# Loading the first tile of a mean-subtract-square kernel in eight pieces, on every eighth partition

## The chip, the core and the metric

The kernel runs on one NeuronCore of a Trainium2 chip. The metric is the device time of one execution in microseconds (us), taken as the median of several runs. One execution is also recorded by the hardware profiler; its record, the trace, is what the pages and tables below are read from. The core's on-chip memory, SBUF, has 128 partitions. Data comes from HBM and goes back to it by DMA, on 16 DMA engines that all DMAs of the core share.

## The reference

For each of the 1024 rows of a 1024 x 4096 float32 matrix, the mean of the row is subtracted from every element and the difference is squared:

```python
def reference(x, axis):                 # x: (1024, 4096) float32, axis = -1
    mean = np.mean(x, axis=axis, keepdims=True)
    return ((x - mean) ** 2).astype(np.float32)
```

Input and output are 16 MiB each (16.78 MB in the units of the profile).

## The kernel before

The matrix is cut into two tiles of 512 rows. In a tile each partition holds four consecutive rows of x, that is 64 KiB in one piece: partition p of tile 0 holds rows 4p to 4p+3. Both tiles are loaded at the start, each by one DMA over all 128 partitions, issued from SyncE (SP). Then, one row per partition at a time, VectorE (DVE) sums the row with negated sign, divides by 4096, and ScalarE (ACT) computes the square of x plus that bias, in place. After each second row the finished half of the tile (128 partitions x 32 KiB, 4 MiB) is stored by one DMA. Both tiles have their own buffer, so nothing waits for a buffer to come free.

```python
    Q = 4                                # rows per partition in a tile
    H = 2                                # rows per store
    ntiles = B // (P * Q)                # 1024 / 512 = 2

    x_t = x.rearrange("(n p q) d -> n p (q d)", p=P, q=Q)
    out_t = out.rearrange("(n p q) d -> n p (q d)", p=P, q=Q)
    # ... pools: one buffer per tile ...

    for i in range(ntiles):
        x_tile = io.tile([P, Q * D], F32)
        nc.sync.dma_start(out=x_tile, in_=x_t[i])          # L43
        tiles.append(x_tile)

    for i in range(ntiles):
        for q in range(Q):
            row = tiles[i][:, q * D:(q + 1) * D]
            # ... neg_sum, neg_mean: [P, 1] each ...
            nc.vector.reduce_sum(out=neg_sum, in_=row,     # L51
                                 axis=mybir.AxisListType.X, negate=True)
            nc.vector.tensor_scalar_mul(out=neg_mean, in0=neg_sum, scalar1=inv_d)   # L54
            nc.scalar.activation(out=row, in_=row,         # L55
                                 func=mybir.ActivationFunctionType.Square,
                                 bias=neg_mean, scale=1.0)
            if q % H == H - 1:
                part = slice((q + 1 - H) * D, (q + 1) * D)
                nc.sync.dma_start(out=out_t[i][:, part], in_=tiles[i][:, part])     # L64
```

Of the kernel before, what the change touches and what calls it, by code (L numbers as in the profile page):

```python
# [2 lines left out]

os.environ.setdefault("NEURON_RT_ULTRASERVER_MODE", "4")

# [4 lines left out]

F32 = mybir.dt.float32


@with_exitstack
def kernel(
    ctx: ExitStack,
    tc: tile.TileContext,
    x: bass.AP,
    axis: bass.AP,
    out: bass.AP,  # L20
):


    nc = tc.nc

    B, D = x.shape
    P = nc.NUM_PARTITIONS
    Q = 4
    H = 2
    assert B % (P * Q) == 0  # L30
    ntiles = B // (P * Q)
    inv_d = 1.0 / float(D)

    x_t = x.rearrange("(n p q) d -> n p (q d)", p=P, q=Q)
    out_t = out.rearrange("(n p q) d -> n p (q d)", p=P, q=Q)

    io = ctx.enter_context(tc.tile_pool(name="io", bufs=ntiles))
    stats = ctx.enter_context(tc.tile_pool(name="stats", bufs=2 * ntiles * Q))

    tiles = []  # L40
    for i in range(ntiles):
        x_tile = io.tile([P, Q * D], F32)
        nc.sync.dma_start(out=x_tile, in_=x_t[i])  # L43
        tiles.append(x_tile)

    for i in range(ntiles):
        for q in range(Q):
            row = tiles[i][:, q * D:(q + 1) * D]
            neg_sum = stats.tile([P, 1], F32)
            neg_mean = stats.tile([P, 1], F32)  # L50
            nc.vector.reduce_sum(  # L51
                out=neg_sum, in_=row, axis=mybir.AxisListType.X, negate=True
            )
            nc.vector.tensor_scalar_mul(out=neg_mean, in0=neg_sum, scalar1=inv_d)  # L54
            nc.scalar.activation(  # L55
                out=row,
                in_=row,
                func=mybir.ActivationFunctionType.Square,
                bias=neg_mean,
                scale=1.0,  # L60
            )
            if q % H == H - 1:
                part = slice((q + 1 - H) * D, (q + 1) * D)
                nc.sync.dma_start(out=out_t[i][:, part], in_=tiles[i][:, part])  # L64


# [1 line left out]
_INS = ['x', 'axis']  # L68
_OUTS = [((1024, 4096), 'float32')]

_NUMBERS = {'axis': -1}


# [26 lines left out]
```

## Time and profile before

| | before |
|---|---|
| time, median of 3 runs (lowest, highest) | 83.3 us (83.25, 83.38) |
| span of the profiled execution | 81.3 us |
| moved by DMA | 16.78 MB read, 16.78 MB written |
| loads | 2 DMAs of 8 MiB |
| stores | 4 DMAs of 4 MiB |
| DVE busy | 35.4 us (44%) |
| ACT busy | 30.7 us (38%) |

The span is the recorded stretch from the first to the last instruction; the measured time is 2.0 us longer. The profile has a line of DMA activity in 40 slices: one digit per slice for the share of time in which the 16 DMA engines had a packet in work, and a line with what they moved, in GB/s. A packet is counted where it ends, so the single GB/s values jump; a table of longer stretches gives the rate more smoothly. In that table each line is a stretch of time with the busy time of the compute engines in it, the DMA share (1.00 is all 16 engines busy all the time) and the rate. "SPq" is the queue of SyncE, from which the DMAs are issued. The chain of waits follows the work that ended last back to the start.

### The profile page before, as it was taken

How to read it: one execution, taken by the hardware profiler on the slowest of the kernel's cores; microseconds unless marked ns; L12 is line 12 of the kernel's file. 1: busy time of each engine (PE TensorE's matmuls, PEld its weight loads, DVE VectorE, ACT ScalarE, POOL GpSimd, SP SyncE). 2: the span in 40 equal slices, each digit the busy share in tenths (PEclk: the TensorE clock that was granted, in tenths of full speed). 3: DMA queues.
4: the chain of work that ended last, by engine and by line, in shares of the span. 5: the costliest groups of instructions: out<-in, count | busy, mean ns of one | idle time of the engine just before them, and what ended most of it. 6: DMA issues, size and time to landing. Idle time of an engine off the chain costs nothing.

```text
span 81.3 us, 79 instructions
## 1 busy us (share of the span) xinstructions
DVE 35.4 (44%) x16; ACT 30.7 (38%) x9; POOL 0.2 (0%) x4
## 2 busy tenths in 40 slices
DVE  0000000000099999999749999999920000000000
ACT  0000000000060005969699930979879980000000
POOL 0000000000000000000000000000000000000000
DMA  9399947999965999992997997997998998898990
GB/s 387 129 516 516 516 193 322 516 516 516 516 290 226 516 516 516 516 483 129 419 516 306 467 516 322 451 516 338 435 516 354 419 516 387 387 516 387 403 500 0
DMA packets 864, 33.55 MB, mean 413 GB/s; under 512 B 96, under 2 KB 96, under 8 KB 96
## 3 DMA queue, kind: packets, MB, share of 16 engines
q1 hardware_dynamic: 864, 33.55, 96.2%
HBM read 16.78 MB, written 16.78 MB: 412 GB/s over the span
## 4 chain that ended last, share of the span: by engine, by line
DMA 50%; DVE 22%; ACT 5%; ACTq 4%; SPq 0%; issue 0%
DMA x_tile<-in_x_dram 50%; DVE neg_sum L51 21%; ACT x_tile L55 5%; ACTq L95 4%; SPq L43 0%; DVE neg_mean L54 0%
## 5 line engine op out<-in xcount | busy, mean ns | idle before, releaser
L51 DVE TENSOR_REDUCE neg_sum<-x_tile 128x1 f32<-128x4096 f32 x8 | 35.0, 4413 | 24.1 <-DMA x_tile<-in_x_dram 24.1
L55 ACT ACTIVATE x_tile<-x_tile,neg_mean 128x4096 f32<-128x4096 f32 x8 | 29.4, 3704 | 13.5 <-DVE neg_mean L54 13.5
L55 ACT ACT_TABLE_LOAD x1 | 1.3, 1283 | 22.5 <-DMA x_tile<-in_x_dram 22.5
L54 DVE TENSOR_SCALAR neg_mean<-neg_sum 128x1 f32<-128x1 f32 x8 | 1.1, 148 | 0.0
L81 POOL MEMSET const-bfloat16-1.0<- 128x1 bf16 x1 | 0.1, 101 | 0.0
L81 POOL MEMSET const-uint8-127<- 128x1 uint8 x1 | 0.1, 101 | 0.0
L81 POOL MEMSET const-float32-0.0<- 128x1 f32 x1 | 0.1, 98 | 0.2 <-issue 0.2
L81 POOL MEMSET const-float32-1.0<- 128x1 f32 x1 | 0.1, 98 | 0.0
## 6 DMA issues: line engine op xcount, KB each, us to landing
out_dram<-x_tile SPq DMA_DIRECT2D x4, 4096.0 KB, 12.9
x_tile<-in_x_dram SPq DMA_DIRECT2D x2, 31.2
```

Source lines behind the costliest of these rows:

```text
L51: nc.vector.reduce_sum(out=neg_sum, in_=row, axis=mybir.AxisListType.X, negate=True)
L54: nc.vector.tensor_scalar_mul(out=neg_mean, in0=neg_sum, scalar1=inv_d)
L55: nc.scalar.activation(out=row, in_=row, func=mybir.ActivationFunctionType.Square, bias=neg_mean, scale=1.0,)
L81: nc = _bacc.Bacc("TRN2", target_bir_lowering=False, num_devices=1)
L95: with _tile.TileContext(nc) as tc:
```

## The change

Tile 0 is now loaded by eight DMAs instead of one. DMA g (g = 0 to 7) reads one contiguous MiB of x, rows 64g to 64g+63, as 16 pieces of 64 KiB, and lays them on the 16 partitions g, g+8, g+16, ..., g+120. So partition 8e+g of tile 0 now holds rows 4(16g+e) to 4(16g+e)+3. The stores of tile 0 follow the same map on the side of HBM, with an access pattern of 16 x 8 x 8192 elements. Tile 1, its load and its stores are as before, and so is all arithmetic. The change is for the HBM side of the load: each DMA reads one unbroken MiB, and its pieces are spread over the whole height of SBUF.

```diff
+    G = 8
+    E = P // G
...
+    x_g = x[:P * Q, :].rearrange("(g e q) d -> g e (q d)", g=G, e=E, q=Q)
+    out_g = out[:P * Q, :].rearrange("(g e q) d -> e g (q d)", g=G, e=E, q=Q)
...
-        nc.sync.dma_start(out=x_tile, in_=x_t[i])
+        if i == 0:
+            for g in range(G):
+                nc.sync.dma_start(out=x_tile[g::G, :], in_=x_g[g])
+        else:
+            nc.sync.dma_start(out=x_tile, in_=x_t[i])
...
-                nc.sync.dma_start(out=out_t[i][:, part], in_=tiles[i][:, part])
+                dst = out_g[:, :, part] if i == 0 else out_t[i][:, part]
+                nc.sync.dma_start(out=dst, in_=tiles[i][:, part])
```

## The prediction, made before the changed kernel ran

> **What bounds the kernel now.** I read the head of the page first: spans, busy shares, and the DMA line in 40 slices.
>
> ```profile
> span 81.3 us, 79 instructions
> DVE 35.4 (44%) x16; ACT 30.7 (38%) x9; POOL 0.2 (0%) x4
> DMA  9399947999965999992997997997998998898990
> q1 hardware_dynamic: 864, 33.55, 96.2%
> HBM read 16.78 MB, written 16.78 MB: 412 GB/s over the span
> ```
>
> No compute engine is busy for half of the span; the DMA engines are busy for 96.2% of it. That alone doesn't say that they set the end, so next I cut the span where loads and stores change over and asked for the table of stretches (columns: stretch, length, busy time of DVE, ACT and POOL, clock, DMA share, GB/s):
>
> ```profile
> 2.20:5.70 3.50, 0.00 (x0) 0.00 (x0) 0.00 (x0) 1.00 0.79 337
> 5.70:22.60 16.90, 0.10 (x1) 0.05 (x1) 0.00 (x0) 1.00 1.00 434
> 22.60:41.90 19.30, 17.68 (x9) 10.43 (x4) 0.00 (x0) 1.00 0.94 407
> 41.90:61.30 19.40, 17.64 (x8) 14.79 (x5) 0.00 (x0) 1.00 1.00 432
> 61.30:80.70 19.40, 0.00 (x0) 5.45 (x2) 0.00 (x0) 1.00 0.94 405
> ```
>
> The load of tile 0 runs at 434 GB/s with share 1.00 once it has started, the stores of tile 0 (41.9 to 61.3) at 432 GB/s, also with share 1.00. (The 407 and 405 come from where packets are counted: each of these stretches also moves 8 MiB in 19.3 or 19.4 us.) So four blocks of 8 MiB follow each other at one rate: 8.389 MB / 434 GB/s = 19.3 us each, 4 x 19.3 = 77.3 us. What is left of 81.3 is about 2.2 us ahead of the first packet, 0.6 us of a slow first round (the stretch to 5.7 us) and about 0.7 us at the end.
>
> The chain of waits and the queue's own waits say whether compute ever delays a store:
>
> ```profile
> 0.73 0.38 SPq L43
> 1.16 40.64 DMA x_tile<-in_x_dram
> 41.83 8.75 DVE neg_sum L51 x2
> ```
> ```profile
> 39.46 27.65 SPq L64 DMA_DIRECT2D out_dram<-x_tile  x4
> ```
>
> The first store is issued at 39.46 us, before the second load has landed (41.8 us), and the last at 66.8 us, while the stores ahead of it still move. The queue never runs dry. The end is set by bytes over rate, not by the DVE and ACT steps that the chain names between 41.8 and 63 us.
>
> [...]
>
> [...]
>
> [...]
>
> [...]
>
> **The change, part by part.**
>
> *Load of tile 0.* Sixteen rows to 16 engines: all engines work, one 64 KiB piece each per DMA. But the partitions are p = 8e + g. [...]Estimate: half of 434, that is 217 GB/s; 8.389 MB / 217 = 38.7 us in place of 19.3: **+19.3 us**, all on the path, as the DMA engines set the end.
>
> *Stores of tile 0.* The HBM side is now 16 x 8 x 8192 elements, the SBUF side 128 x 8192. [...]Two stores, 8.389 MB, at 216 instead of 432 GB/s: **+19.4 us**. This step rests on my reading of how such a pattern is dealt out, so it is less sure than the first.
>
> *More DMAs.* Seven more issues of about 0.4 us (0.38 us above) are done by 0.73 + 8 x 0.4 = 4 us, beside transfers that last to 40 us: 0 on the path. The built program has eight completion semaphores for its DMAs, so the load of tile 1, the ninth DMA, waits until the first MiB has landed, at 6 to 8 us; by then seven more MiB are in the queue, at least 17 us of work. 0 on the path. DVE's first reduction waits for eight semaphores in place of one, also beside the load of tile 1.
>
> *Packets.* Load pieces stay at 64 KiB and store pieces at 32 KiB, so their number stays 256 + 512; there are 7 x 16 = 112 more completion packets. In the page all packets together, completions too, fill 96.2%, and no gap shows where two DMAs meet; I count 0.1 us.
>
> *Does a late load starve the stores?* Tile 0 lands at 22.5 + 19.3 = 41.8 us, tile 1 at 61.1. The first store would be issued at 39.5 + 19.3 = 58.8, still ahead of 61.1. Tile 1's last store is issued near 66.8 + 19.4 = 86.2, while the stores of tile 0 move until 61.1 + 38.8 = 99.9. No new gap. Sum: 81.3 + 19.3 + 19.4 + 0.1 = 120.1 us of span, 122.1 us of time.
>
> **The rivals.**
>
> *Only the loads slow down.* [...]the time is 83.3 + 19.4 = 102.7 us. For it: the SBUF side of the store is still 128 partitions. Against: the HBM side no longer is.
>
> *Engines drift apart.* [...]Then the load costs 10 to 15 us more and the stores as well: 103 to 113 us. Against: equal pieces and a start within half a microsecond make them march together.
>
> [...]nothing changes but the issue: 83.3 us, or 82.7 if contiguous reads also remove the slow first round (0.6 us). [...]A gain over 2% (1.7 us) would need more than the whole of that slow round[...].
>
> **Range and chances.** I give both conflicts 0.6 (116 to 124 us), one alone or drift 0.25 (98 to 113), no conflict 0.13, faster 0.02. [...]I say 121 us. The range, 100 to 124.5, takes in the loads-only case. Faster 0.02, same 0.13, slower 0.85.
>
> **What would show it.** Right: from about 6 to 41 us the DMA share stays at 1.00 while the rate is near 217 GB/s, and DVE starts near 42 instead of 22.5 us; from 42 to 61 the load of tile 1 is back at 434; from 61 to 100 the stores of tile 0 show 216; from 100 on 432 again. DVE and ACT durations (4413 and 3704 ns) don't change. Wrong: 434 GB/s from 6 us on[...]; 432 from 61 us on[...]; a rate between that rises towards the end of the first load (drift); a low DMA share, which would mean waiting for issue or semaphores instead of slow packets.

## The result: half as long again

The changed kernel takes 124.84 us (median of 6 runs, 123.86 to 125.06), the kernel before 83.32 us (6 runs, 83.25 to 83.4). The ratio is 1.4966, with a 95% interval of 1.4918 to 1.5013: 41.5 us more.

First the head of its page, to be held against the head shown in the prediction:

```profile
span 123.3 us, 97 instructions
DVE 35.4 (29%) x16; ACT 30.7 (25%) x9; POOL 0.2 (0%) x4
q1 hardware_dynamic: 976, 33.56, 95.1%
HBM read 16.78 MB, written 16.78 MB: 272 GB/s over the span
```

DVE and ACT did the same work in the same time. The same bytes went through 16 DMA engines that were as busy as before (95.1%, before 96.2%), but the rate fell from 412 to 272 GB/s. This is the line to remember: an engine that is held up counts as busy. Each packet just takes longer: in the records of single packets a 64 KiB piece of tile 0 takes 5.11 us, before 2.42. The extra 112 packets are the completions of seven more DMAs, 7 x 16.

The timeline of the changed kernel (columns: start, length, then what) says when the tiles arrived:

```profile
0.73 5.08 SPq L51 DMA_DIRECT2D x_tile<-in_x_dram  x8
8.85 0.35 SPq L53 DMA_DIRECT2D x_tile<-in_x_dram  x1
44.42 8.75 DVE L61 TENSOR_REDUCE neg_sum<-x_tile 128x1 f32<-128x4096 f32 x2 [44.42 <-DMA x_tile<-in_x_dram]
61.38 27.35 SPq L75 DMA_DIRECT2D out_dram<-x_tile  x4
63.45 8.74 DVE L61 TENSOR_REDUCE neg_sum<-x_tile 128x1 f32<-128x4096 f32 x2 [1.32 <-DMA x_tile<-in_x_dram]
```

DVE gets tile 0 at 44.42 us instead of 22.50, tile 1 at 63.45 instead of 41.83. Tile 0 comes 21.9 us late, and tile 1 as good as keeps that delay (21.6 us): between the two lie 19.0 us, before 19.3. The load of tile 1 is issued late, at 8.85 us, because it waits for the first MiB (3.0 us in the queue's own waits), but with seven MiB still queued that costs nothing. The first store is issued at 61.38 us, ahead of the last load again.

The table of stretches of the changed kernel, cut at those points, shows the rates (last column GB/s, before it the DMA share). A packet counts in the stretch in which it starts, not, as said above, in which it ends:

```profile
6.80:42.50 35.70, 0.00 (x0) 0.00 (x0) 0.00 (x0) 1.00 1.00 206
42.50:62.70 20.20, 17.71 (x8) 9.36 (x4) 0.00 (x0) 1.00 0.99 415
62.90:82.00 19.10, 17.71 (x8) 14.79 (x5) 0.00 (x0) 1.00 0.93 206
82.00:102.40 20.40, 0.00 (x0) 6.37 (x2) 0.00 (x0) 1.00 1.00 259
102.40:122.30 19.90, 0.00 (x0) 0.00 (x0) 0.00 (x0) 1.00 0.83 357
120.10:123.30 3.20, 0.00 (x0) 0.00 (x0) 0.00 (x0) 1.00 0.02 10
```

The last stretch of the same length in the kernel before:

```profile
78.10:81.30 3.20, 0.00 (x0) 0.00 (x0) 0.00 (x0) 1.00 0.38 164
```

Tile 0 is loaded at 206 GB/s with share 1.00. Tile 1 loads at 415. The stores of tile 0 begin at 206 and come to 259 in their second half (which holds some of tile 1's stores). In the last line is something new: in the last three microseconds only a few engines still start a packet.

### The profile page after: what moved, and what is told of

Its sections match the earlier page's. It is cut to its first block, busy times and chain, and to the rows that moved or that the text cites. A ratio compares the mean times of both kernels' runs of the same rounds, so it can differ in the third digit from the quotient of the medians.

```text
span 123.3 us, 97 instructions
## 1 busy us (share of the span) xinstructions
DVE 35.4 (29%) x16; ACT 30.7 (25%) x9; POOL 0.2 (0%) x4
## 3 DMA queue, kind: packets, MB, share of 16 engines
q1 hardware_dynamic: 976, 33.56, 95.1%
## 4 chain that ended last, share of the span: by engine, by line
DMA 32%; DVE 29%; SPq 3%; ACT 3%; ACTq 3%; another core or an unknown queue 1%; issue 0%; DVEq 0%
DMA x_tile<-in_x_dram 32%; DVE neg_sum L61 28%; SPq L51 3%; ACT x_tile L65 3%; ACTq L106 3%; DVE neg_mean L64 0%; DVEq L61 0%
```

## The experiments

The theory: the partitions that the 16 engines work on at one moment set the rate. Sixteen with a step of 8, as in the load, get half of the 434 GB/s; the stores get as little because, by my estimate, their pattern leads the engines to such partitions as well. The recorded texts call that a conflict. Why such partitions should be slow no trace shows. The rivals: the HBM side (all engines inside one MiB), the number of DMAs, and, for the stores, engines brought out of step by the load. In all of them only tile 0's transfers are edited, starting from the kernel before; times stand beside runs of the kernel before on the same chip (83.23 to 83.29 us). The ratios leave out single executions more than 1.5% above the fastest of their kernel, so they can differ a little from the quotient of two medians.

### The loads alone, with the old rows

```diff
-        nc.sync.dma_start(out=x_tile, in_=x_t[i])
+        if i == 0:
+            for g in range(8):
+                nc.sync.dma_start(out=x_tile[g::8, :], in_=x_t[0][g::8, :])
```

> The load of tile 0 is eight DMAs onto partitions g, g+8, ..., as in the changed kernel, but each partition keeps the rows it had before, so a DMA reads 16 pieces of 64 KiB that lie 512 KiB apart in HBM in place of one unbroken MiB; the stores are those of the kernel before. [...]the reads don't matter, the partitions do. DVE starts near 44.4 us as in the changed kernel, the stores run at 432 GB/s, the time is 83.3 + 21.9 = 105.2 us. Rival, HBM locality (16 engines reading inside one MiB slow each other down): DVE starts near 22.5 us and the time is near 83.5 us. Rival, number of DMAs: [...]the runs on 128 partitions and on 16 partitions in a row tell it apart.

Measured: 104.77 us, 1.258 times the kernel before (1.255 to 1.260), 21.5 us more. From its timeline and its table of stretches:

```profile
44.41 8.74 DVE L55 TENSOR_REDUCE neg_sum<-x_tile 128x1 f32<-128x4096 f32 x2 [44.41 <-DMA x_tile<-in_x_dram]
```
```profile
6.80:42.50 35.70, 0.00 (x0) 0.00 (x0) 0.00 (x0) 1.00 1.00 207
62.70:82.00 19.30, 17.71 (x8) 15.00 (x5) 0.00 (x0) 1.00 1.00 433
```

Reads 512 KiB apart or in one unbroken MiB: DVE starts at 44.41 or 44.42 us. So the order of reads in HBM has no part in the loss. The stores here are at 433 GB/s, so what slowed them in the changed kernel is not the load before them.

### The same MiBs on 16 partitions in a row

```diff
+                nc.sync.dma_start(out=x_tile[16 * g:16 * g + 16, :],
+                                  in_=x_t[0][16 * g:16 * g + 16, :])
```

> The load of tile 0 is eight DMAs of one contiguous MiB each, onto 16 partitions in a row (16g to 16g+15), rows and stores as before. [...]tile 0 lands near 80 us, the time is 141 to 147 us. Rivals, HBM locality or number of DMAs: the reads and the count are those of the changed kernel, so DVE starts at 44.4 us and the time is near 105 us.

Measured: 139.07 us, 1.670 times (1.666 to 1.674). The stretch that lies inside the load of tile 0:

```profile
10.00:75.00 65.00, 0.00 (x0) 0.00 (x0) 0.00 (x0) 1.00 0.98 111
```

Same count of DMAs, same size, each reading one unbroken MiB as in the changed kernel, and the rate about halves again. It is a little better than the 141 to 147 us that I expected: 111 GB/s is 0.54 of the changed kernel's 206, where 206 is 0.47 of 434.

### Eight DMAs over all 128 partitions

```diff
+            for g in range(8):
+                c = slice(2048 * g, 2048 * g + 2048)
+                nc.sync.dma_start(out=x_tile[:, c], in_=x_t[0][:, c])
```

> The load of tile 0 is eight DMAs of one MiB each, all over 128 partitions with 8 KiB a partition, rows and stores as before. [...]434 GB/s, DVE starts near 22.6 us, the time is 83.2 to 84 us. Rival, number of DMAs (issue, completion, the wait of the ninth for the first): the time rises by a good part of the 21.9 us by which tile 0 came late in the changed kernel, to 95 us or more.

Measured: 84.75 us, 1.018 times (1.016 to 1.020). The number of DMAs is not the cause. The 1.5 us are more than I had allowed; its timeline says where they are lost:

```profile
22.80 4.42 DVE L56 TENSOR_REDUCE neg_sum<-x_tile 128x1 f32<-128x4096 f32 x1 [0.36 <-DMA x_tile<-in_x_dram]
43.19 8.74 DVE L56 TENSOR_REDUCE neg_sum<-x_tile 128x1 f32<-128x4096 f32 x2 [15.78 <-DMA x_tile<-in_x_dram]
```

The last piece of tile 0 comes only 0.3 us late, tile 1 then 1.4 us late. So the loss falls into the load of tile 1, which is unchanged, but here the first store is issued at 21.23 us and waits behind it. In the records of single packets the last 16 pieces of that load take 3.35 to 3.77 us each instead of 2.42. That the waiting stores slow them is a guess, not shown.

### The stores alone

```diff
+                    dst = out[:P * Q, :].rearrange("(g e q) d -> e g (q d)",
+                                                   g=8, e=16, q=Q)[:, :, part]
```

> Loads as in the kernel before, stores of tile 0 with the 16 x 8 x 8192 pattern of the changed kernel, so the rows of tile 0 come out in another order. Theory: [...]near 216 GB/s instead of 432, and they alone cost 18.5 to 20.5 us, with the ends of the 16 engines spread by 2 to 3 us: 102 to 104 us. If the extra of this run and that of the loads alone add up to the 41.5 us of the changed kernel, the two are separate. Rival: the stores of the changed kernel were slow because the conflict of the load had brought the engines out of step; then this run is near 83.5 us.

Measured: 103.26 us, 1.236 times (1.229 to 1.244), 20.0 us more. 21.5 + 20.0 = 41.5: the two parts add up to the whole of the changed kernel. Its table of stretches, first the load, then the stores of tile 0, then the end:

```profile
5.70:22.60 16.90, 0.00 (x0) 0.00 (x0) 0.00 (x0) 1.00 1.00 434
42.50:80.00 37.50, 17.34 (x8) 19.96 (x6) 0.00 (x0) 1.00 0.98 247
97.00:101.10 4.10, 0.00 (x0) 0.00 (x0) 0.00 (x0) 1.00 0.06 24
```

The stores are slow behind a load at full rate, but at 247 GB/s, not 216 (the stretch holds some of tile 1's stores too). And the end is ragged: share 0.06 over the last 4.1 us. The engines drift apart in these stores: until 67 us their 32 KiB packets take anything from 1.2 to 2.8 us, before 1.21. The packets fill 93.4% of the span of 101.1 us, 94.4 us of each engine; before they filled 78.2 of 81.3. So the packets cost 16.2 us more, not 19.4. But 6.7 us are idle instead of 3.1, and these 3.6 us lie at the end, where the engines that are done don't take over what is left to the others.

### Loads on two kinds of partition sets in one kernel

```diff
+            spans = [slice(32 + j, 96, 4) for j in range(4)]
+            spans += [slice(j, 32, 2) for j in range(2)]
+            spans += [slice(96 + j, 128, 2) for j in range(2)]
+            for g in range(8):
+                nc.sync.dma_start(out=x_tile[spans[g], :], in_=x_g[g])
```

> The load of tile 0 is eight DMAs of one contiguous MiB on 16 partitions each, as in the changed kernel; the first four go to partitions 32+j, 36+j, ..., 92+j (j = 0 to 3)[...], the last four to every second partition of 0 to 31 and of 96 to 127[...]. Stores of the kernel before, so the rows of tile 0 come out in another order. [...]the first 4 MiB at 434 GB/s (until about 12.5 us), the next 4 MiB at 205 GB/s (20.5 us more), DVE starts near 33.3 us, the time is 83.3 + 10.8 = 94.1 us. Rivals, HBM locality or DMAs of 16 partitions as such: no difference between the halves, DVE starts near 44.4 us, the time is near 105 us.

Measured: 94.41 us, 1.133 times (1.131 to 1.136). Timeline, then the stretches of the first four and the last four DMAs:

```profile
33.84 8.74 DVE L59 TENSOR_REDUCE neg_sum<-x_tile 128x1 f32<-128x4096 f32 x2 [33.84 <-DMA x_tile<-in_x_dram]
```
```profile
5.70:12.60 6.90, 0.00 (x0) 0.00 (x0) 0.00 (x0) 1.00 1.25 427
12.60:33.30 20.70, 0.00 (x0) 0.00 (x0) 0.00 (x0) 1.00 0.92 212
```

This is the clearest of the runs. Eight DMAs of one kind, 16 partitions and one unbroken MiB each; four run at 427 GB/s and four at 212, and only the choice of partitions sets them apart. (The first share is over 1 because whole packets are counted where they start.) In the records of single packets the first set takes 2.42 us for 64 KiB once started, the second mostly 5.11, the same as in the changed kernel.

### Stores on the same two kinds of sets

```diff
+                    for g in range(8):          # the same spans
+                        nc.sync.dma_start(out=out_g[g][:, part],
+                                          in_=tiles[i][spans[g], part])
```

> Loads of the kernel before; each of the two stores of tile 0 is cut into eight DMAs of 16 partitions, [...]each writes 16 pieces of 32 KiB inside one MiB of HBM (64 KiB apart), as in the changed kernel, so the rows of tile 0 come out in another order. [...]in each half store 2 MiB at 432 GB/s (4.9 us) and 2 MiB at about 207 GB/s (10.1 us), so 5.3 us more for each, the time is near 93.5 to 95 us. Rival, HBM writes inside one MiB are slow: no difference between the DMAs, near 103 us. Rival, small DMAs wait for issue: the DMA share falls below 1.

Measured: 95.15 us, 1.140 times (1.132 to 1.147), just over what I expected. The two halves of the first store, then of the second:

```profile
41.90:46.60 4.70, 4.64 (x2) 4.70 (x2) 0.00 (x0) 1.00 1.10 397
46.60:57.00 10.40, 10.40 (x5) 6.50 (x3) 0.00 (x0) 1.00 0.91 233
57.00:61.00 4.00, 2.67 (x3) 3.32 (x2) 0.00 (x0) 1.00 1.09 418
61.00:71.00 10.00, 0.00 (x0) 5.88 (x2) 0.00 (x0) 1.00 0.96 239
```

Fast, slow, fast, slow, with the same kind of HBM writes throughout. The partitions matter for reading SBUF (397 and 418 GB/s against 233 and 239) as they do for writing it (427 against 212), and 16 engines writing inside one MiB of HBM are not slow.

### Contiguous reads without the conflict

```diff
+            x_q = x[:P * Q, :].rearrange("(q p) d -> q p d", p=P, q=Q)
+            for q in range(Q):
+                nc.sync.dma_start(out=x_tile[:, q * D:(q + 1) * D], in_=x_q[q])
...
+                    out_q = out[:P * Q, :].rearrange("(q p) d -> p q d", p=P, q=Q)
+                    # store out_q[:, q + 1 - H:q + 1, :]
```

> What the change was for, without the conflict: the load of tile 0 is four DMAs of two contiguous MiB each, over all 128 partitions, one row of 16 KiB per partition; the stores of tile 0 follow that map. [...]contiguous reads bring nothing, [...]and all stays at the rate of before: 83.0 to 84.5 us, though DVE starts near 8 us because its first reduction needs only the first DMA. Rival, contiguous reads are worth something: below 82 us.

Measured: 84.54 us, 1.016 times (1.013 to 1.018). What the change was for brings nothing even without its price. Nor does compute that starts at 8.33 us: the queue of bytes is as long as before. The 1.3 us lost look like those of the run with eight DMAs over 128 partitions: here too stores wait early, and the last 16 pieces of tile 1's load take 2.70 to 3.63 us.

### A store pattern of 8 x 16

```diff
+                    dst = out[:P * Q, :].rearrange("(g e q) d -> e g (q d)",
+                                                   g=16, e=8, q=Q)[:, :, part]
```

> As the run of the stores alone, but the HBM side of the stores of tile 0 is 8 x 16 x 8192 elements: partition 16e+g holds rows of block (g, e), e = 0 to 7, g = 0 to 15 (rows of tile 0 come out in another order). [...]only 8 engines work, [...]the 8.39 MB take 81 us in place of 19.4, time near 145 us. If they drift apart as in the run with 16 x 8, up to a third less: not under 120 us. Rival, the scattered HBM writes are what costs: as with 16 x 8, near 103 us. Rival, 8 engines with no conflict[...] (217 GB/s): also 103 us, but with half of the packets missing from the second eight engines, so the DMA share would be 0.5; the rate per busy engine tells it.

Measured: 144.89 us, 1.734 times (1.723 to 1.746). From its page, and a stretch early in tile 0's stores:

```profile
DMA packets 848, 33.55 MB, mean 233 GB/s; under 512 B 80, under 2 KB 80, under 8 KB 80
```
```profile
44.00:58.00 14.00, 14.00 (x6) 10.07 (x3) 0.00 (x0) 1.00 0.49 108
```

80 completion packets where the kernel before has 96, 16 for each DMA: that fits two DMAs with 8 completions each, on 8 engines only. Share 0.49 is half of the engines, and at 108 GB/s each of the eight gets 13.5, half of the 27.1 of an engine before. So these eight are slow themselves; at the rate of before they would reach 8 x 27.1 = 217 GB/s, by estimate. The time fits too (145 was expected). Over 43 to 119 us the share is 0.65 and the rate 179 GB/s: by my reading the other eight engines have gone on to tile 1's stores, and the rates mix.

### The load in two queues

```diff
+                issuer = nc.sync if g < 4 else nc.scalar
+                issuer.dma_start(out=x_tile[g::8, :], in_=x_t[0][g::8, :])
```

> The loads of the run with partitions 8e+g and old rows, but g = 0 to 3 are issued from SyncE and g = 4 to 7 from ScalarE[...]. If [...]half of the engines start with the one and half with the other, the conflict goes: tile 0 lands near 23 us, time 83.5 to 86 us. If all engines alternate in step, both sets still take turns: 104 to 105.5 us as with one queue. In between if they drift.

Measured: 103.86 us, 1.249 times (1.246 to 1.252). The engines stay in step: in the records of single packets all 16 take a piece of the one queue, then all 16 a piece of the other. So they alternate between the partitions of g = 0 to 3 and those of g = 4 to 7, and the conflict stays: DVE starts at 43.39 us. The 0.9 us saved on the 104.77 of one queue are in the packets, which take 4.93 us in place of 5.11.

### One load DMA with the pattern of the stores

```diff
+            x_e = x[:P * Q, :].rearrange("(g e q) d -> e g (q d)", g=8, e=16, q=Q)
+            nc.sync.dma_start(out=x_tile, in_=x_e)
```

> The load of tile 0 is one DMA over 128 partitions whose HBM side is 16 x 8 x 16384 elements, the pattern of the changed kernel's stores; stores of the kernel before, so the rows of tile 0 come out in another order. Theory[...]: the load is slow with one DMA too, DVE starts near 44 us and the time is near 105 us, or some us less if the engines drift apart as they do in the stores. Rival ([...]the slow stores have another cause): DVE starts near 22.5 us, time near 83.4 us.

Measured: 104.61 us, 1.257 times (1.255 to 1.259); from its timeline:

```profile
44.10 8.74 DVE L55 TENSOR_REDUCE neg_sum<-x_tile 128x1 f32<-128x4096 f32 x2 [44.10 <-DMA x_tile<-in_x_dram]
```

One DMA over 128 partitions is as slow as eight over 16, if its HBM side leads with a dimension of 16. So neither is one DMA over 128 partitions safe by itself: what counts, by the theory, is which partitions the engines touch at the same moment. Loads of this pattern keep in step (after the first round every piece takes 4.90 to 5.13 us); stores of it drift.

## Why the prediction was wrong, and how much of it was right

Both slowdowns came, and their size was off: 124.84 us were measured, 122.1 summed, 121 said.

*What bounds the kernel.* Right. The run with contiguous reads over all 128 partitions (84.54 us) shows that neither a better read order nor earlier compute brings anything. A slip without effect: the first packet starts at 1.7 us, not 2.2, and after the last there is over 1 us, not 0.7.

*The load: the step that failed.* "Estimate: half of 434, that is 217 GB/s". The half was an estimate that no trace of the kernel before could test. Measured: 206 GB/s, 12.9 per engine instead of 434 / 16 = 27.1; a 64 KiB packet took 5.11 us, 2.11 times 2.42, not twice. The term was 19.3 and measured 21.5 (the loads alone). That is 2.2 of the 2.7 us by which the worked sum of 122.1 fell short.

*The stores.* Predicted +19.4, measured +20.0, but the closeness is partly luck. The rival "engines drift apart", to which I gave little, came true here and made the stores themselves cheaper (alone, 16.2 us more per engine, not 19.4), and then the uneven engines gave 3.6 us back in idle time at a ragged end, which I had not foreseen. In the changed kernel the same sum, against the run of the loads alone, is 17.9 us in packets and 2.3 idle. My reading of how the pattern is dealt out is not shown: which engine took which partition the trace does not say. The runs with 8 x 16 and with one load DMA show that the pattern sets the rate, 108 and 207 GB/s.

*More DMAs, late loads, starved stores.* Right: 0 on the path. The eight issues took 5.08 us, not 4, and still lay beside transfers.

*The range.* I said 121 us, 1.1 less than the sum, on an estimate that no run here shows, and the upper edge stood only 2.4 us above the sum. I allowed for drift and good luck, not for worse than half; in a running stream the packets took 2.11 times as long.

*No conflict; only the loads slow down.* Both fell; both parts are there, and they add up.

No version run here beats the kernel before. After its first round of packets it moves its bytes at 432 to 434 GB/s.

## What to carry to other kernels

Before splitting a DMA by partitions, measure the rate on the very set of partitions that each piece takes, with a stretch inside the transfer: DMA share 1.00 at half the usual GB/s was here the mark of packets that take twice as long (5.11 us against 2.42). One DMA over all 128 partitions with the same 128 leading on the HBM side ran at 432 to 434 GB/s; a leading dimension of 16 on the HBM side about halved that (207 in the load), and in a store one of 8 quartered it (108). When a rate is expected to halve, allow in the range for worse than half (here 206 of 434).

## What the hardware showed that I had not expected

Sixteen partitions with a step of 8 got 206 GB/s, less than half of the 434 on all 128; 16 in a row got 111, a little more than a quarter. The figure for 16 in a row is from loads alone. And it matters what came before: in the records of single packets of the changed kernel the pieces of the fifth DMA (g = 4) take 4.94 to 4.95 us, those of the second to fourth and of the sixth to eighth 5.11 to 5.12. A change of partitions from g = 3 to g = 4 thus came with a shorter round, and that fits the gain of the two queues, where every round is such a change (4.93 us). What causes either stays open.

Stores in conflict drift apart and loads don't: with the same 16 x 8 pattern the load held 207 GB/s with engines in step, the stores reached 247 and ended unevenly. Why is open too.
